# Ten float32r weight blocks of a float32 encoder trunk: the rounded copy fetched by a second transfer instead of made by ScalarE

## The chip, the core and the metric

The kernel runs on one core of one Trainium2 chip. The metric is the device time of one execution in microseconds, lower is better; a comparison uses the median over rounds. The float32r matrix products run on TensorE, whose granted clock was full in the profiled execution (0.998 of full speed over the span).

## What is computed

A bidirectional encoder of two layers works on two groups of requests with the same weights: 256 prompt tokens and 512 sample tokens, width 1024, all in float32. Both groups are handled as six tiles of 128 tokens; attention stays within its group. Each layer is a token mixer and then a SwiGLU channel mixer of inner width 2816, each between two RMS norms:

```python
for i in range(DEPTH):                                   # DEPTH = 2
    h = rms_norm(x, norm_mix_pre[i])
    if i % 2 == 0:
        m = window_gqa_sink(h, a_w_in, a_w_o, a_sinks)   # the first mixer
    else:
        m = diff_attention(h, b_w_in, b_w_o, ...)        # the second mixer
    x = x + rms_norm(m, norm_mix_post[i])
    h = rms_norm(x, norm_ffn_pre[i])
    x = x + rms_norm(swiglu(h, w_gate_up[i], w_down[i]), norm_ffn_post[i])
```

Only the first mixer matters for the change. It has 16 query heads of 64 in four groups, one key and value head per group, rotary positions on queries and keys, a window of 128 tokens to both sides, and a learned sink logit per head. For each query block of 128 tokens and each head: scores against two or three key blocks, the row maximum with the sink, the exponential, the sum with the sink's term, the division, and the product with the values; then the output projection `o @ w_o`.

## The kernel before

**Three products for one.** A weight product is computed to nearly float32 precision from float32r operands. Each operand is split into a high part, which is the operand rounded to float32r, and a low part, which is the operand minus the high part. A product is then three matmuls: high by high, high by low, low by high. In the code a block of weights has a raw tile `wraw` (float32, 128x1024), a high tile `whi` and a low tile `wlo`. `two_parts` makes them: ScalarE copies `wraw` into `whi`, which rounds, and VectorE subtracts `whi` from `wraw` into `wlo`. The activations have `hhi` and `hlo`, made in the same way, for the tiles 0 to 2 (half 0) and 3 to 5 (half 1).

**How the weights flow.** All weight blocks stand in one list in the order of use, called units. Units 0 to 3 are the weights of values and of the first keys (128x768 each). Units 4 to 12 are nine blocks of 128x1024 for eight pairs of query heads and the second pair of key heads: q0, q1, q2, q3, k8, q4, q5, q6, q7. Units 13 to 20 are the output projection; the channel mixer's units follow. `load` issues the transfer of a raw block on SyncE's queue; there are two buffers for `wraw`, and a buffer comes free when VectorE has made the low part. There are five buffers each (`RING = 5`) for `whi` and `wlo`, so unit i takes the buffer of unit i-5 and can only be written when TensorE has finished with that one. `prepare(upto)` emits the split of the units up to a number; `free` calls it when a unit's last product has been emitted.

**The order of the work.** The first mixer walks a list of projections ("fills"): values and first keys of the six tiles with q0 between, then each query block by halves, then the key block k8 by halves. Into the matmuls of the fills it places, at written positions, the attention's steps of heads already projected. A step is: scores (`sc`, TensorE), mask and row maximum (VectorE, a custom instruction that writes `y_e` and `negm`), exponential (ScalarE), reciprocal of the sum (`den`, VectorE), the scaling of two heads by it (`y_e`; one head on VectorE, one on ScalarE), transposes (`tpe`, TensorE), their copy (`eT`, ScalarE), and the product with the values (`poa`, TensorE). A projected query block is turned by its rotary positions: ScalarE copies it out of PSUM to `xqa`, two transfers issued by GpSimd exchange the rows of the two rotary halves, VectorE multiplies by the tables and adds (`zqa`), and ScalarE and VectorE split the result into `qa`. The tile framework's scheduler then sets the order of the instructions on each engine; each engine executes its instructions strictly in that order. `tc.issue_after` keeps instructions behind a named one in that order.

**GpSimd's queue** in the first mixer holds the row factors of the norms (`rstd_pre`), the exchanging transfers (`xqa`, `xka`) and the copies of a key block to the other half of the partitions (`ka`), in one order. A transfer whose condition isn't met holds whatever stands behind it.

The change touches the end of `prepare`, where every unit is split. Its line before is `two_parts(hi[:, :n], lo[:, :n], src[:, :n])`. `raw_src[r][0]` is the block's address in DRAM.

Of the kernel before, what the change touches and what calls it, by code (L numbers as in the profile page):

```python
# [9 lines left out]
F32 = mybir.dt.float32  # L10
# [3 lines left out]
ALU = mybir.AluOpType  # L14
# [9 lines left out]
NPAIR = NCH // 2  # L24
DOWN = ("b11", "t1", "t2", "b22", "t3", "t4")
RING = 5
NGRP = (NPAIR + 1) // 2
RAW = {"w": 2, "y": 2, "tt": 2, "rb": 2}
AHEAD = 6
# [58 lines left out]
def trunk(  # L88
# [22 lines left out]
    nc = tc.nc  # L111
# [22 lines left out]
    for at, step, mult in ((0, 1, -1), (2 * P, -1, 1)):  # L134
        nc.gpsimd.affine_select(
            out=mask[:, at:at + P], in_=mask[:, at:at + P], compare_op=ALU.is_ge, fill=MASK, base=0,
# [45 lines left out]
    raw_src, units = [], []  # L182
# [13 lines left out]
    def ffn_units(layer):  # L196
# [13 lines left out]
        for kind, quarter, home in (  # L210
                ("plain", (1, 0), "w"), ("b11", (0, 0), "tt"), ("t1", (0, 1), "rb"), ("t2", (1, 1), "w"),
                ("b22", (1, 1), "w"), ("t3", (1, 0), "w"), ("t4", None, None)):
            for g in range(NGRP):
                n = 512 * min(2, NPAIR - 2 * g)
# [22 lines left out]
    state = {"dma": 0, "split": 0, "used": 0, "w": 0, "y": 0, "tt": 0, "rb": 0, "behind": None, "after": None, "hold": False}  # L237
# [10 lines left out]
    def fetch(upto=None):  # L248

        while state["dma"] < (len(raw_src) if upto is None else upto):  # L250
            i = state["dma"]
            src, n, home = raw_src[i]
            if upto is None and (state[home] >= RAW[home] or home in quarters and dpool[0] is None):
                break
            if RAW["w"] <= i < 4:
                raw = first.tile([P, 768], F32, name=f"wraw{i}")
            elif home == "y":
                raw = new_y(f"wraw{i}")
            elif home in quarters:
                small_one = n < 1024  # L260
                raw = dpool[0].tile(
                    [P, n], F32, tag=home + "s" * small_one, name=f"{home}{i}", bufs=1 if small_one else NPAIR // 2)
            else:
                raw = wpool.tile([P, 1024], F32, tag="wraw", name=f"wraw{i}", bufs=RAW["w"])
            if not RAW["w"] <= i < 4:
                state[home] += 1
            load(raw[:, :n], src)
            raws[i] = raw
            state["dma"] += 1

    def two_parts(hi, lo, src):
        state["raw_hi"] = nc.scalar.copy(out=hi, in_=src)  # L272
        state["raw_lo"] = nc.vector.tensor_tensor(out=lo, in0=src, in1=hi.bitcast(F32), op=ALU.subtract)  # L273

    def prepare(upto):

        while state["split"] < min(upto, len(units)):
            i = state["split"]
            kind, r, n = units[i]
            if kind != "t4":  # L280
                fetch((r[1] if kind in ("t32", "t14") else r) + 1)
            hi = wpool.tile([P, 1024], F32R, tag="whi", name=f"whi{i}", bufs=RING)
            lo = wpool.tile([P, 1024], F32R, tag="wlo", name=f"wlo{i}", bufs=RING)
            if kind in ("plain", "gate"):
                src = raws[r]
            elif kind == "t14":
                src = raws[r[0]]
            elif kind in DOWN:
# [11 lines left out]
                src = {"b11": raw, "b22": raw, "t3": rb}.get(kind, tt)  # L300
            else:
# [10 lines left out]
                src = u  # L312
            with ExitStack() as after:
                if state["after"] is not None:
                    after.enter_context(tc.issue_after(state["after"].ins))
                if 4 <= i < 8:
                    after.enter_context(tc.issue_after(state["rstd"].ins))
                    after.enter_context(tc.issue_after(state["scaled"].ins))
                two_parts(hi[:, :n], lo[:, :n], src[:, :n])
            if kind == "t14" and units[i - 2][0] == "plain":  # L320
                state["t14_lo"] = state["raw_lo"]
            if kind == "b22":
# [22 lines left out]
    def take(n):  # L345

        i = state["used"]
        state["used"] += n
        prepare(i + n)
        return [parts.pop(j) for j in range(i, i + n)]  # L350

    def free(n_live):

        if not state["hold"]:
            prepare(state["used"] - n_live + RING)

# [779 lines left out]
    def ffn(layer, later, comb, cpool, cstack, ostack, gains):  # L1136
        sub = 2 * layer + 1
        at_hand = [
            dram.tile([P, 7, min(2, NPAIR - 2 * g), HALF], F32, name=f"act{layer}_{g}") for g in range(NGRP)]
        a_ops = {  # L1140
# [182 lines left out]
        with ExitStack() as st:  # L1323
# [53 lines left out]
            def one(p, g, into, first=False, last=False):  # L1377
                wk = {g: take(1)[0]}
                run(p, [g], wk, range(3), into, first, last)
                acts.used(1)  # L1380
                free(0)

            def whole(p, into, events):

                for g in range(NGRP):
                    one(p, g, into, p in (0, 1, 2) and g == 0, g == NGRP - 1)
                    for e in events.get(g, ()):
# [18 lines left out]
                3: [do(stage, 0, 3), do(stage, 1, 2)]}  # L1406
            for g in range(NGRP - 2):
                one(5, g, V)
                for e in events[g]:
                    e()  # L1410
            gs = range(NGRP - 2, NGRP)
            wk = dict(zip(gs, take(2)))
# [274 lines left out]
```

## Time and profile before

| | us |
|---|---|
| median of three timed runs | 1646.34 (1643.15 to 1646.58) |
| profiled execution, its own time | 1643.85 |
| its span, first to last instruction | 1642.1 |
| TensorE busy in the span | 1607.4 |
| VectorE busy | 1202.0 |
| ScalarE busy | 949.5 |
| GpSimd busy | 164.3 |

The profiled execution lies 2.5 us under the median of the timed runs and within their range. Its time is 1.75 us more than its span. In the views that follow PE is TensorE's matmuls, PEld its weight loads, DVE VectorE, ACT ScalarE, POOL GpSimd and SP SyncE; "SPq" and "POOLq" are transfers issued on those queues. A row of a timeline gives the start, the duration, the engine, the line, the operation with what it writes and reads, and in brackets how long the engine had been idle just before and what it waited for. All line numbers in profile rows are those of the kernel before.

### The profile page before, as it was taken

Reading aid. Unit: us, or ns where it says so; the run is one execution under the profiler, and the core shown is the slowest. Engines: PE = TensorE matmul, PEld = TensorE weight load, DVE = VectorE, ACT = ScalarE, POOL = GpSimd, SP = SyncE. Lnnn points to the kernel's source line nnn. Section 1 sums busy time; section 2 is a strip of 40 time slices with the busy share of each in tenths; the row PEclk is TensorE's granted clock in tenths of the full one; section 3 lists DMA queues with packets and bytes.
Section 4 is the critical chain, followed back from the end, with each engine's and each line's share of the span. In section 5 each row is a group of like instructions: output and inputs, shape, how many; then the busy total and the mean of one; then the engine's idle time right before and its main releaser. Section 6 shows DMA issues by size and latency. Waiting matters only on the chain. (4 is left out here: it accounts for less than half of the span.)

```text
span 1642.1 us, 24438 instructions
## 1 busy us (share of the span) xinstructions
PE 1607.4 (98%) x9055; PEld 1489.1 (91%) x9055; DVE 1202.0 (73%) x2076; ACT 949.5 (58%) x2009; POOL 164.3 (10%) x251
## 2 busy tenths in 40 slices
PE   7999999999999999999999999999999999999997
PEld 7888878999999998888999999888989999998886
DVE  6778857886666766988685886847886667656985
ACT  6789976644444444556475676766644444444553
POOL 1111001000000000001220251421000000000010
PEclk9999999999999999999999999999999999999999
DMA  5322205453433247666432322504443433347674
GB/s 201 97 70 58 97 15 176 170 170 111 144 111 122 100 138 269 237 235 209 130 97 71 100 72 85 148 15 178 155 158 123 144 112 103 114 143 255 215 242 159
DMA packets 71943, 227.83 MB, mean 139 GB/s; under 512 B 8912, under 2 KB 17296, under 8 KB 71568
## 3 DMA queue, kind: packets, MB, share of 16 engines
q1 hardware_dynamic: 55008, 178.82, 32.5%
q0 software_dynamic: 16672, 47.20, 9.5%
q8 instruction: 71, 1.16, 0.3%
q14 instruction: 48, 0.39, 0.1%
q10 hardware_dynamic: 144, 0.26, 0.0%
HBM read 166.47 MB, written 42.86 MB: 127 GB/s over the span
## 5 line engine op out<-in xcount | busy, mean ns | idle before, releaser
L273 DVE TENSOR_TENSOR wlo<-wraw,whi 128x1024 fp32r<-128x1024 f32 (+2 forms) x171 | 203.0, 1190 | 189.7 <-ACT whi L272 188.8
L272 ACT CAST whi<-wraw 128x1024 fp32r<-128x1024 f32 (+2 forms) x171 | 174.9, 1026 | 126.2 <-PE py L371 61.6
L370 PE MATMUL py<-hhi,whi 128*128 128x384 f32 x480 | 161.2, 336 | 1.0 <-ACT u L1177 0.9
L372 PE MATMUL py<-hhi,wlo 128*128 128x384 f32 x480 | 160.4, 334 | 0.0
L371 PE MATMUL py<-hlo,whi 128*128 128x384 f32 x480 | 160.4, 334 | 0.0
L358 ACT CAST hhi<-araw 128x768 fp32r<-128x768 f32 (+1 forms) x74 | 57.6, 783 | 93.3 <-DMA araw<-act 93.0
L370 PEld LDWEIGHTS py<-hhi,whi 128*128 128x128 f32 x480 | 90.1, 188 | 3.4 <-ACT u L1177 2.4
L372 PE MATMUL pv<-whi,hlo 128*128 128x512 f32 (+1 forms) x240 | 92.2, 384 | 0.1
L370 PE MATMUL pv<-whi,hhi 128*128 128x512 f32 (+1 forms) x240 | 92.3, 384 | 0.0
L371 PE MATMUL pv<-wlo,hhi 128*128 128x512 f32 (+1 forms) x240 | 92.1, 384 | 0.0
L371 PEld LDWEIGHTS py<-hlo,whi 128*128 128x128 f32 x480 | 90.1, 188 | 0.0
L372 PEld LDWEIGHTS py<-hhi,wlo 128*128 128x128 f32 x480 | 90.1, 188 | 0.0
L359 DVE TENSOR_TENSOR hlo<-araw,hhi 128x768 fp32r<-128x768 f32 (+1 forms) x74 | 65.2, 890 | 32.8 <-ACT hhi L358 32.5
L1220 POOL DMA_DIRECT2D act<-st x22 | 19.3, 878 | 628.6 <-DVE st L1219 628.6
L370 PE MATMUL po<-whi,hhi 128*128 128x512 f32 x192 | 78.5, 409 | 0.0
L1017 ACT ACTIVATE be<-bsc,bmx 128x512 f32<-128x512 f32 (+1 forms) x96 | 58.7, 615 | 30.4 <-DVE bmx L1015 29.8
L371 PE MATMUL px<-hlo,whi 128*128 128x384 f32 x224 | 75.0, 335 | 0.7 <-DVE hlo L359 0.7
L370 PE MATMUL px<-hhi,whi 128*128 128x384 f32 x224 | 75.3, 336 | 0.2 <-ACT hhi L358 0.2
L371 PE MATMUL po<-wlo,hhi 128*128 128x512 f32 x192 | 75.3, 392 | 0.0
L372 PE MATMUL po<-whi,hlo 128*128 128x512 f32 x192 | 75.2, 392 | 0.0
L372 PE MATMUL px<-hhi,wlo 128*128 128x384 f32 x224 | 74.9, 335 | 0.0
L1015 DVE TENSOR_REDUCE bmx<-bsc 128x1 f32<-128x512 f32 (+1 forms) x96 | 55.2, 594 | 11.3 <-PE bsc L1011 10.9
(315 smaller groups left out, 4897.9 us busy)
## 6 DMA issues: line engine op xcount, KB each, us to landing
wraw<-in_wgu SPq DMA_DIRECT2D x60, 512.0 KB, 4.5
act<-st POOLq DMA_DIRECT2D x22, 1344.0 KB, 6.5
araw<-act SPq DMA_DIRECT2D x70, 384.0 KB, 3.9
y_wraw<-in_wgu SPq DMA_DIRECT2D x40, 512.0 KB, 3.7
wraw<-in_wd SPq DMA_DIRECT2D x40, 512.0 KB, 3.7
xd<-x SPq DMA_DIRECT2D x18, 512.0 KB, 3.1
x<-xd SPq DMA_DIRECT2D x18, 512.0 KB, 4.3
wraw<-in_wo SPq DMA_DIRECT2D x16, 512.0 KB, 3.7
```

The costliest lines, as they stand in the source:

```text
L272: state["raw_hi"] = nc.scalar.copy(out=hi, in_=src)
L273: state["raw_lo"] = nc.vector.tensor_tensor(out=lo, in0=src, in1=hi.bitcast(F32), op=ALU.subtract)
L358: state["hi"] = nc.scalar.copy(out=hi, in_=src)
L359: state["lo"] = nc.vector.tensor_tensor(out=lo, in0=src, in1=hi.bitcast(F32), op=ALU.subtract)
L370: nc.tensor.matmul(out, ah, bh, start=start and i == 0, stop=False, skip_group_check=more)
L371: nc.tensor.matmul(out, ah, bl, start=False, stop=False, skip_group_check=more)
L372: state["mm"] = nc.tensor.matmul(out, al, bh, start=False, stop=stop and i == last, skip_group_check=more)
L1015: nc.vector.tensor_reduce(out=mx, in_=s, axis=AX.X, op=ALU.max, negate=True)
L1017: nc.scalar.activation(out=e[:, :n * P], in_=s, func=AF.Exp, bias=mx, accum_out=den[:, c:c + 1])
L1220: nc.gpsimd.dma_start(out=at_hand[c // 4][:, :, c // 2 % 2], in_=out.pop(c // 2))
```

## The change

For units 4 to 13 the high part is no longer made by ScalarE. GpSimd issues a second transfer of the same block from DRAM, whose destination is the float32r tile `whi`, so that the transfer itself rounds. VectorE's subtraction is as before, but now reads a `whi` that came by transfer. These are the nine blocks of queries and keys and the first block of the output projection. The raw block still comes by SyncE's transfer, since the low part needs it. All other units are split as before.

```diff
--- before.py
+++ after.py
@@ -24,6 +24,7 @@
 NPAIR = NCH // 2
 DOWN = ("b11", "t1", "t2", "b22", "t3", "t4")
 RING = 5
+N_PLAIN_A = 14
 NGRP = (NPAIR + 1) // 2
 RAW = {"w": 2, "y": 2, "tt": 2, "rb": 2}
 AHEAD = 6
@@ -316,7 +317,12 @@
                 if 4 <= i < 8:
                     after.enter_context(tc.issue_after(state["rstd"].ins))
                     after.enter_context(tc.issue_after(state["scaled"].ins))
-                two_parts(hi[:, :n], lo[:, :n], src[:, :n])
+                if 4 <= i < N_PLAIN_A:
+                    nc.gpsimd.dma_start(out=hi[:, :n], in_=raw_src[r][0])
+                    state["raw_lo"] = nc.vector.tensor_tensor(
+                        out=lo[:, :n], in0=src[:, :n], in1=hi[:, :n].bitcast(F32), op=ALU.subtract)
+                else:
+                    two_parts(hi[:, :n], lo[:, :n], src[:, :n])
             if kind == "t14" and units[i - 2][0] == "plain":
                 state["t14_lo"] = state["raw_lo"]
             if kind == "b22":
```

The scheduler sets a new order around this. In the pieces below a number in a name like `whi5` is the unit; `xqa1_0` is the rotary exchange of query block 1, half 0; `den`, `negm` and `y_e` carry group, tile and first head.

GpSimd's queue at the first query blocks, before and then now:

```order
L415 TENSOR_TENSOR rstd_pre0_5_395<-rstd_pre0_5_395,mhalf_101 128x1
L653 DMA xqa0_0_481<-xqa0_0_481 64x384 x2
L653 DMA xqa1_0_716<-xqa1_0_716 64x384 x2
L653 DMA xqa0_1_787<-xqa0_1_787 64x384 x2
L653 DMA xqa1_1_868<-xqa1_1_868 64x384 x2
L653 DMA xqa2_0_971<-xqa2_0_971 64x384 x2
L653 DMA xqa3_0_1077<-xqa3_0_1077 64x384 x2
```

```order
L421 TENSOR_TENSOR rstd_pre0_4_331<-rstd_pre0_4_331,mhalf_101 128x1
L421 TENSOR_TENSOR rstd_pre0_5_395<-rstd_pre0_5_395,mhalf_101 128x1
L659 DMA xqa0_0_481<-xqa0_0_481 64x384 x2
L321 DMA whi5_596<-in_waf 128x1024
L321 DMA whi6_615<-in_waf 128x1024
L321 DMA whi7_635<-in_waf 128x1024
L321 DMA whi8_647<-in_waf 128x1024
L659 DMA xqa1_0_716<-xqa1_0_716 64x384 x2
L321 DMA whi9_781<-in_waf 128x1024
L659 DMA xqa0_1_787<-xqa0_1_787 64x384 x2
L321 DMA whi10_862<-in_waf 128x1024
```

The ten transfers stand between the exchanges: unit 4 ahead of the third row factor (not shown), units 5 to 8 in a row ahead of the second query block's exchange, unit 9 and unit 10 one exchange later each. Further on, units 11, 12 and 13 stand ahead of the copies of the first `ka` half, of `xqa3_1` and of `xka8_1`.

TensorE where unit 5 is used for the first time, at the end of the last value projection (`pkva5`), before and then now:

```order
L372 MATMUL pkva5_589<-whi3_205,hlo1_113 128x384
L370 MATMUL pqa1_0_665<-hhi0_110,whi5_596 128x384
L371 MATMUL pqa1_0_665<-hlo0_112,whi5_596 128x384
L372 MATMUL pqa1_0_665<-hhi0_110,wlo5_597 128x384
L783 MATMUL sc0_0_1_669<-ka0_296,qa0_0_520 128x256 x2
L370 MATMUL pqa1_0_665<-hhi0_110,whi5_596 128x384
L371 MATMUL pqa1_0_665<-hlo0_112,whi5_596 128x384
L372 MATMUL pqa1_0_665<-hhi0_110,wlo5_597 128x384
```

```order
L378 MATMUL pkva5_589<-whi3_205,hlo1_113 128x384
L376 MATMUL pqa1_0_665<-hhi0_110,whi5_596 128x384
L377 MATMUL pqa1_0_665<-hlo0_112,whi5_596 128x384
L789 MATMUL sc0_0_1_669<-ka0_296,qa0_0_520 128x256 x2
L742 MATMUL tka4_683<-ident_r_86,sp4_579 128x128 x4
L789 MATMUL sc0_1_0_690<-ka0_296,qa0_0_520 128x256 x2
L378 MATMUL pqa1_0_665<-hhi0_110,wlo5_597 128x384
L376 MATMUL pqa1_0_665<-hhi0_110,whi5_596 128x384
```

The first matmul with the low part of unit 5 has moved behind two scores and a transpose.

VectorE at the same place, before and then now:

```order
L609 TENSOR_TENSOR kr4_580<-kr4_580 128x128
L273 TENSOR_TENSOR wlo5_597<-wraw5_178,whi5_596 128x1024
L729 TENSOR_TENSOR sp4_579<-kr4_580,sp4_579 128x128 x2
L792 ISA y_e0_0_0_624,negm0_0_0_625<-sc0_0_0_621,mask_91,nsink_107 128x256
L792 ISA negm0_0_0_625 128x1
L273 TENSOR_TENSOR wlo6_616<-wraw6_367,whi6_615 128x1024
L603 TENSOR_TENSOR kr5_656<-pkva5_589,cos_sb_99 128x128
L606 TENSOR_TENSOR kr5_656<-pkva5_589,sin_sb_100 128x64 x2
L792 ISA y_e0_0_0_624,negm0_0_0_625<-sc0_0_1_669,mask_91,nsink_107 128x256
L792 ISA negm0_0_0_625 128x1
L609 TENSOR_TENSOR kr5_656<-kr5_656 128x128
L801 TENSOR_TENSOR den0_0_0_626<-negm0_0_0_625,sink_106 128x2
```

```order
L615 TENSOR_TENSOR kr4_580<-kr4_580 128x128
L735 TENSOR_TENSOR sp4_579<-kr4_580,sp4_579 128x128 x2
L798 ISA y_e0_0_0_624,negm0_0_0_625<-sc0_0_0_621,mask_91,nsink_107 128x256
L798 ISA negm0_0_0_625 128x1
L322 TENSOR_TENSOR wlo5_597<-wraw5_178,whi5_596 128x1024
L609 TENSOR_TENSOR kr5_656<-pkva5_589,cos_sb_99 128x128
L612 TENSOR_TENSOR kr5_656<-pkva5_589,sin_sb_100 128x64 x2
L322 TENSOR_TENSOR wlo6_616<-wraw6_367,whi6_615 128x1024
L615 TENSOR_TENSOR kr5_656<-kr5_656 128x128
L798 ISA y_e0_0_0_624,negm0_0_0_625<-sc0_0_1_669,mask_91,nsink_107 128x256
L798 ISA negm0_0_0_625 128x1
L735 TENSOR_TENSOR sp5_655<-kr5_656,sp5_655 128x128 x2
```

`wlo5` stood ahead of `sp4` and the first maximum and now stands behind them; `wlo6` follows it closely. `wlo7` and `wlo8`, which are not shown, keep their places to within a few rows.

VectorE at unit 13, in the attention of group 1, before and then now:

```order
L659 TENSOR_TENSOR zqa3_1_1428<-zqa3_1_1428,xqa3_1_1424 128x384
L792 ISA y_e1_2_2_1499,negm1_2_2_1500<-sc1_2_2_1496,mask_91,nsink_107 128x256
L792 ISA negm1_2_2_1500 128x1
L803 TENSOR_TENSOR den1_1_2_1456<-den1_1_2_1456 128x2
L792 ISA y_e1_2_2_1499,negm1_2_2_1500<-sc1_2_3_1519,mask_91,nsink_107 128x256
L792 ISA negm1_2_2_1500 128x1
L804 RECIPROCAL den1_1_2_1456<-den1_1_2_1456 128x2
L273 TENSOR_TENSOR wlo13_1514<-wraw13_1298,whi13_1513 128x1024
L668 TENSOR_TENSOR qa3_1_1485<-zqa3_1_1428,qa3_1_1485 64x384 x2
L806 TENSOR_SCALAR y_e1_1_2_1454<-y_e1_1_2_1454,den1_1_2_1456 128x256
L792 ISA y_e1_3_0_1543,negm1_3_0_1544<-sc1_3_0_1540,mask_91,nsink_107 128x384
```

```order
L665 TENSOR_TENSOR zqa3_1_1428<-zqa3_1_1428,xqa3_1_1424 128x384
L809 TENSOR_TENSOR den1_1_2_1456<-den1_1_2_1456 128x2
L798 ISA y_e1_2_2_1499,negm1_2_2_1500<-sc1_2_3_1519,mask_91,nsink_107 128x256
L798 ISA negm1_2_2_1500 128x1
L810 RECIPROCAL den1_1_2_1456<-den1_1_2_1456 128x2
L807 TENSOR_TENSOR den1_2_2_1501<-negm1_2_2_1500,sink_106 128x2
L812 TENSOR_SCALAR y_e1_1_2_1454<-y_e1_1_2_1454,den1_1_2_1456 128x256
L674 TENSOR_TENSOR qa3_1_1485<-zqa3_1_1428,qa3_1_1485 64x384 x2
L798 ISA y_e1_3_0_1543,negm1_3_0_1544<-sc1_3_0_1540,mask_91,nsink_107 128x384
L798 ISA negm1_3_0_1544 128x1
L661 TENSOR_TENSOR zka8_1_1534<-xka8_1_1530,ropea0_238 128x384
L322 TENSOR_TENSOR wlo13_1514<-wraw13_1298,whi13_1513 128x1024
```

The scaling of `y_e1_1_2` stood behind `wlo13` and behind the split of `qa3_1`, and now stands ahead of both. `wlo12`, which is not shown, stood ahead of the scaling of `y_e1_2_0` and of both maxima of `y_e1_1_2`; now it stands behind that scaling and between the two maxima.

## The prediction

> **What bounds the kernel now.** I read first the page's head with the busy time of each engine, then the busy time by stretches (the columns are the stretch, its length, and PE, PEld, DVE, ACT and POOL busy, granted clock, DMA share, GB/s), then TensorE's waits between 20 and 200 us.
>
> ```profile
> span 1642.1 us, 24438 instructions
> ...
> PE 1607.4 (98%) x9055; PEld 1489.1 (91%) x9055; DVE 1202.0 (73%) x2076; ACT 949.5 (58%) x2009; POOL 164.3 (10%) x251
> ...
> 0.00:60.00 60.00, 51.68 (x311) 49.96 (x312) 39.23 (x96) 38.65 (x91) 7.23 (x19) 1.00 0.52 176
> 60.00:76.00 16.00, 12.63 (x81) 11.94 (x79) 14.31 (x46) 12.40 (x34) 2.20 (x4) 1.00 0.28 91
> 76.00:112.00 36.00, 35.87 (x240) 31.02 (x239) 28.12 (x97) 31.69 (x92) 5.80 (x10) 1.00 0.19 49
> 112.00:126.00 14.00, 11.83 (x77) 10.24 (x78) 11.19 (x41) 11.73 (x35) 2.20 (x4) 1.00 0.32 103
> 126.00:200.00 74.00, 72.26 (x474) 61.01 (x472) 61.02 (x213) 68.21 (x197) 10.07 (x18) 1.00 0.23 71
> 200.00:1642.10 1442.10, 1423.15 (x7883) 1324.94 (x7879) 1048.14 (x1588) 786.85 (x1565) 136.84 (x196) 1.00 0.44 144
> ...
> PE tpe L824 <- DVE y_e L806: 2.4, 3, 2.0
> PE tpe L824 <- DVE den L801: 2.1, 2, 1.9
> PE sc L783 <- DVE qa L668: 1.4, 1, 1.4
> ```
>
> TensorE bounds the kernel at full clock. The change lies in the first 200 us; the order of the instructions behind them is the old one, so a shift made there is carried to the end as it is. In those 200 us TensorE can lose or win only at places where it waits: three groups of waits hold 2.4 + 2.1 + 1.4 = 5.9 us, and all three end at VectorE. None ends at ScalarE's rounding. Between 76 and 112 us TensorE is busy for 35.87 of 36 us. So the change is worth what it moves at three places (63, 73 and 121 us), less what a late transfer costs.
>
> **The change part by part.** What goes: ten roundings of 1.05 us on ScalarE. What comes: ten transfers of 512 KB on GpSimd's queue. The subtractions stay on VectorE, but wait now for a landing.
>
> ```profile
> L272 ACT CAST whi<-wraw x10: 1031/1048/1064, 25.4 to 115.8; 128x1024 fp32r<-128x1024 f32 x10
> ...
> act<-st POOLq DMA_DIRECT2D x22, 1344.0 KB, 6.5
> kb<-kb POOLq DMA_DIRECT2D x32, 192.0 KB, 3.1
> wraw<-in_waf SPq DMA_DIRECT2D x9, 512.0 KB, 3.7
> ...
> L653 POOL DMA_DIRECT2D xqa<-xqa x32: 552/552/718, 34.8 to 195.4; - x32
> ...
> DMA to landing us min/median/max: 1.8/2.6/4.1
> ```
>
> *The landing.* No transfer that rounds 512 KB is in the trace. By GpSimd's queue 192 KB land after 3.1 us and 1344 KB after 6.5; on the line between them 512 KB land after 3.1 + 3.4 x 320/1152 = 4.0 us, close to the 3.7 us of the same block on SP's queue. I take 4.0; the ends are 3.1 (rounding and size cost nothing) and 6.5 (it costs as much as the largest transfer). Where the rounding has another price it is a rival below. Ten issues at 0.55 to 0.72 us of GpSimd time are 5.5 to 7.2 us; GpSimd is busy for 7.23 + 2.20 + 5.80 + 2.20 + 10.07 = 27.5 of 200 us, and that idle time hides them: 0. The exchanges behind them in its queue wait for a copy of a query block, which comes later than the release of the buffer in every place that the order shows; without that cover each exchange would be late by one issue, 0.7 us.
>
> *Unit 5, TensorE at 48 us.* The rows are ScalarE's rounding of unit 5 and TensorE's first use.
>
> ```profile
> 44.60 1.05 ACT L272 CAST whi<-wraw 128x1024 fp32r<-128x1024 f32 x1 [0.67 <-PE pkva L372]
> 48.14 0.33 PE L370 MATMUL pqa<-hhi,whi 128*128 128x384 f32 x1
> 50.46 0.46 PE L736 MATMUL tka<-ident_r,sp 128*128 128x128 f32 x4
> 50.76 0.47 PE L783 MATMUL sc<-ka,qa 128*128 128x256 f32 x2
> 51.07 0.34 PE L370 MATMUL pqa<-hhi,whi 128*128 128x384 f32 x1
> ```
>
> The rounding waited for TensorE to release the buffer (44.60). The transfer is released at the same moment and lands at 44.6 + 4.0 = 48.6, 0.46 after TensorE wants it: **+0.5**. The subtraction (1.22, quoted below) then ends at 49.8. Until its first use TensorE now has two products with the high part (0.17 each from start to start), two scores and a transpose (0.30 and 0.31 from the starts above): 1.27 us, which covers it. With 3.1 us the term is 0, with 6.5 it is 44.6 + 6.5 - 48.14 = +3.0. What is late next is the end of query block 1, half 0, and with it the exchange on which the wait at 63 us hangs, so I count the delay in full.
>
> *Units 9 and 10, TensorE at 63 and 73 us.* ScalarE and VectorE rows around the two waits:
>
> ```profile
> 60.97 1.05 ACT L666 CAST qa<-zqa 64x384 fp32r<-64x384 f32 x2 [1.39 <-DVE zqa L659]
> 61.26 1.22 DVE L273 TENSOR_TENSOR wlo<-wraw,whi 128x1024 fp32r<-128x1024 f32 x1
> 62.04 0.49 ACT L651 ACTIVATE xqa<-pqa 128x384 f32<-128x384 f32 x1
> 63.11 0.51 PE L783 MATMUL sc<-ka,qa 128*128 128x256 f32 x2 [1.45 <-DVE qa L668]
> 65.65 1.03 ACT L272 CAST whi<-wraw 128x1024 fp32r<-128x1024 f32 x1
> 66.76 0.56 DVE L658 TENSOR_TENSOR xqa<-xqa,ropea 128x384 f32<-128x384 f32 x1 [1.39 <-DMA xqa<-xqa]
> 68.11 1.22 DVE L273 TENSOR_TENSOR wlo<-wraw,whi 128x1024 fp32r<-128x1024 f32 x1
> 70.53 0.48 DVE L792 CUSTOM_DVE_ANT_0 y_e<-sc,mask,nsink 128x256 f32<-128x256 f32 x1
> 73.39 0.64 PE L824 MATMUL tpe<-ident,y_e 128*128 128x128 f32 x4 [1.92 <-DVE den L801]
> ```
>
> The subtraction of unit 9 (61.26) stood ahead of the split of `qa1_0`, which could begin at 62.48. It now stands four rows behind that split's group, in the gap of 1.39 ahead of 66.76. The split can begin when ScalarE's rounding ends, 62.02: 0.46 earlier. The gap, longer by that, is 1.85 and takes the 1.22, so the row at 66.76 comes 0.63 earlier if its exchange has landed. It will have: its copy (62.04) now stands ahead of the rounding of `qa1_0`, where ScalarE idled for 1.39. The wait at 73 us follows VectorE, busy 14.31 of 16 us here, so both waits together give **-0.6**. The subtraction of unit 10 stood at 68.11 and now stands behind two maxima (0.48 each) and a split (1.14): 70.2 - 0.6 = 69.6. Its buffer is free at 65.65 at the latest and the block lands at 69.65: 0. With 6.5 it lands at 72.15, and VectorE, with everything behind it in its order, is 2.6 us late, TensorE too.
>
> *Units 12 and 13, TensorE at 121 us.* VectorE, ScalarE and TensorE rows:
>
> ```profile
> 115.76 1.05 ACT L272 CAST whi<-wraw 128x1024 fp32r<-128x1024 f32 x1 [0.17 <-PE pqa L371]
> 116.61 0.56 DVE L658 TENSOR_TENSOR xqa<-xqa,ropea 128x384 f32<-128x384 f32 x1 [1.80 <-DMA xqa<-xqa]
> 118.63 1.21 DVE L273 TENSOR_TENSOR wlo<-wraw,whi 128x1024 fp32r<-128x1024 f32 x1
> 118.69 0.33 PE L370 MATMUL pqa<-hhi,whi 128*128 128x384 f32 x1
> 119.22 0.34 PE L370 MATMUL pqa<-hhi,whi 128*128 128x384 f32 x1
> 119.87 1.14 DVE L668 TENSOR_TENSOR qa<-zqa,qa 64x384 fp32r<-64x384 f32 x2
> 121.04 0.35 DVE L806 TENSOR_SCALAR y_e<-y_e,den 128x256 f32<-128x256 f32 x1
> 121.54 0.63 PE L824 MATMUL tpe<-ident,y_e 128*128 128x128 f32 x4 [1.99 <-DVE y_e L806]
> ```
>
> The scaling at 121.04 stood behind the subtraction of unit 13 and a split and now stands ahead of both: 121.04 - (121.04 - 118.63) = 118.63. The subtraction of unit 12 goes later, into the gap of 1.80 ahead of 116.61. The transposes start 0.5 after the scaling does, as before: 119.15 instead of 121.54. TensorE was ready at 121.54 - 1.99 = 119.55 and is now ready four matmuls earlier (three take 119.22 - 118.69 = 0.53, four 0.7), at 118.85. A wait of 0.3 stays: **-1.7**. The release of unit 13's buffer is at 115.76, its landing at 119.8, and its subtraction now stands behind 118.63 + 0.35 + 1.14 and more, past 120: 0. What goes back: the next transposes wait for the scaling of `y_e1_2_2`, which now stands behind that subtraction (1.21); and behind 126 us ScalarE is busy for 68.21 of 74 us, so that TensorE, early, finds work that isn't ready. Nothing in the trace says how much; between 0 and 1.7 I take half: **+0.85**.
>
> *ScalarE's ten microseconds.* Seven of the ten roundings end before 67 us, where ScalarE is busy for 38.65 of 60 and 12.40 of 16 us; the other three are at 100 to 116 us, where the waits end at VectorE. What they free is idle time, beyond the order already counted: 0; rival two prices it otherwise. *Memory.* The second reading adds 5.2 MB. The DMA share is 0.52 up to 60 us and 0.19 to 0.32 up to 200; the room left hides it, and no wait of TensorE quoted above ends at a transfer: 0, or, without that room, the longer landing already bounded.
>
> The sum: 0.46 - 0.63 - 1.7 + 0.85 = -1.0. With 3.1 us and nothing given back it is -0.63 - 1.7 = -2.3; with 6.5 it is 3.0 - 0.63 + 2.6 - 1.7 + 0.85 = +4.1. The profiled execution took 1643.85 us by its own time, so it becomes 1642.9; the median of the runs is 2.5 us above it, so the forecast on the median is 1646.34 - 1.0 = **1645.4**, from 1644.0 to 1650.4 by the ends.
>
> **The rivals.** *One, slower: the rounding transfer is slow.* If it rounds at half the speed of the plain block, it lands after 2 x 3.7 = 7.4 us. Then unit 5 holds TensorE at 48 us for 44.6 + 7.4 - 48.14 = 3.9, and unit 10 holds VectorE at 73 us for 65.65 + 7.4 - 69.6 = 3.5, with the scalings and splits behind it: 3.9 + 3.5 - 0.63 - 1.7 + 0.85 = +5.9, 1652.2. Each further microsecond costs two, so from a landing of 6.2 us on the result is slower by more than 3.3. For it: no row shows a transfer with rounding, and units 5 and 10 have no slack left at 4.0 us (-0.46 and -0.05). Against it: the plain rows, at 3.7 and 6.5.
>
> *Two, faster: ScalarE's relief counts.* From 60 to 200 us ScalarE is busy for 12.40 + 31.69 + 11.73 + 68.21 = 124.0 of 140 us, and what VectorE waits with often comes from it (exponentials, roundings of a split). If its shorter queue gives back three quarters of the 5.9 us of waits, it is -4.4: 1641.9. Against it: those waits are named as VectorE's, and seven of ten roundings stood in idle time.
>
> *Three: the gain is handed on whole.* If the work behind 126 us holds TensorE until the old time, and units 5 and 10 cancel, nothing is left: 1646.3.
>
> [...]
>
> **How the numbers follow.** 0.2%, 3.3 us, is about what a measurement of this kernel can tell from no change. The forecast gets 0.36, rival one 0.22, two 0.25, three 0.12, four 0.05. Faster is rival two, 0.25; slower is rival one, 0.22; the rest, 0.53, is within 0.2%. The forecast's own range is 1644.0 to 1650.4. The range for all takes in rivals one and two about to their prices, so that some 0.2 stays outside: 1641.0 to 1652.2.
>
> **What would show it.** In the changed kernel's trace: ten transfers of `whi` with a landing near 4 us (rival one: 6.2 or more); TensorE's wait for `whi` at 48 us near 0.5; waits at 63 and 73 us of 1.45 and 1.92 together shorter by about 0.6; the transposes of 121 us with a wait of 0.3 instead of 1.99, and new waits of about 0.9 in all between 124 and 200 us. A busy time of TensorE that changes, or a difference behind 200 us, would mean that the argument looked in the wrong place.

## The result, and the profile after

The changed kernel takes 1641.95 us in the median, against 1645.84 us for the kernel before (22 runs each). The ratio is 0.998 with a 95% interval of 0.9974 to 0.9986: 3.3 us faster, between 2.3 and 4.3. One run of the changed kernel was disturbed (2676 us) and is not in the ratio. The forecast was -1.0 us. Its own range, 1644.0 to 1650.4 us, did not hold the time; the range that takes in the rivals, from 1641.0 us on, did. The end of this section and the last experiment show that 2.1 us of the gain, about two thirds, come from a place that the prediction did not look at.

The page's head, TensorE's waits between 20 and 210 us, and the busy time by stretches of the changed kernel (columns as before):

```profile
span 1641.9 us, 24431 instructions
...
PE 1610.2 (98%) x9055; PEld 1491.5 (91%) x9055; DVE 1200.9 (73%) x2076; ACT 941.0 (57%) x1999; POOL 170.9 (10%) x261
...
PE tpe L830 <- DVE y_e L812: 2.3, 2, 2.1
PE tpe L830 <- ACT y_e L813: 1.0, 3, 0.4
PE poa L845 <- ACT eT L836: 0.8, 2, 0.4
PE sc L789 <- DVE qa L674: 0.6, 1, 0.6
PE pqa L376 <- DMA whi<-in_waf: 0.5, 1, 0.5
...
60.00:76.00 16.00, 13.36 (x82) 12.75 (x81) 14.14 (x47) 11.74 (x35) 4.24 (x8) 0.94 0.60 206
74.00:77.50 3.50, 3.35 (x12) 3.38 (x13) 2.54 (x11) 3.45 (x10) 1.09 (x2) 0.51 0.35 132
112.00:126.00 14.00, 13.32 (x86) 11.97 (x85) 12.11 (x43) 10.89 (x34) 2.89 (x6) 1.00 0.53 157
126.00:200.00 74.00, 72.49 (x474) 61.30 (x473) 61.13 (x214) 68.67 (x199) 9.94 (x18) 1.00 0.23 72
```

The span is only 0.2 us shorter than in the profile of before, although the timed runs differ by 3.3. The profiled execution of before (1643.85 us) lies 2.0 under that kernel's median. This one (1643.67 us) is 1.7 over its own, and the row from 74 to 77.5 us gives one reason: there the granted clock was 0.51. A single pair of traces can't carry the comparison here. Rows have to be matched place by place.

The rows of TensorE and VectorE at the places of the prediction:

```profile
49.58 0.41 PE L376 MATMUL pqa<-hhi,whi 128*128 128x384 f32 x1 [0.47 <-DMA whi<-in_waf]
63.73 0.51 PE L789 MATMUL sc<-ka,qa 128*128 128x256 f32 x2 [0.56 <-DVE qa L674]
74.15 1.09 PE L830 MATMUL tpe<-ident,y_e 128*128 128x128 f32 x4 [2.08 <-DVE y_e L812]
120.57 0.60 PE L830 MATMUL tpe<-ident,y_e 128*128 128x128 f32 x4
122.82 1.22 DVE L322 TENSOR_TENSOR wlo<-wraw,whi 128x1024 fp32r<-128x1024 f32 x1 [0.72 <-DMA whi<-in_wo]
...
L659 POOL DMA_DIRECT2D xqa<-xqa x32: 527/545/657, 35.6 to 196.0; - x32
...
DMA to landing us min/median/max: 3.8/5.1/5.8
```

The first exchange starts at 35.6 us instead of 34.8. This lead of 0.8 us of the kernel before is there from 16 us on, before any product uses a changed unit, so it isn't the change: by the clock records of the two traces the full clock was granted 1.8 us later in this execution (16.0 against 14.2 us). Counted without it, the scores at 63 us come 0.2 us earlier than before (63.73 against 63.11), the transposes at 73 us at the same time (74.15 against 73.39), and the transposes at 121 us no longer wait at all (120.57 against 121.54). The last row is the time from issue to landing of the ten new transfers: 5.1 us in the median, not 4.0.

The half-clock stretch begins at 74.0, at the end of a wait of 2.08 us, and costs about 1.5 us: the shift against the kernel before grows from 0.8 at 74 us to 2.2 at 80. Among the fourteen traces of this study such a stretch stands at this place in four (the changed kernel twice, order_only, combo6), behind 121 us in one, and nowhere in the first mixer in the other nine. It lasts 3.41 us each time. Waits of much the same length brought it in some executions and not in others: the 2.08 us here did, the 1.99 us at 121 us in the trace of before did not. The part on the clock below shows when.

The last two outputs of the kernel before, and then of the changed kernel:

```profile
1636.25 0.34 SPq L564 DMA_DIRECT2D ys<-x  x1
1636.92 0.37 ACTq L564 DMA_DIRECT2D ys<-x  x1
```

```profile
1638.20 0.34 SPq L570 DMA_DIRECT2D ys<-x  x1
1638.87 0.37 ACTq L570 DMA_DIRECT2D ys<-x  x1
```

From the issue of the last output to the end of the span it was 1642.1 - 1636.9 = 5.2 us; now it is 1641.9 - 1638.9 = 3.0. No instruction there was changed. This is 2.1 us, the larger part of the gain. The traces also hold instructions that the views don't count as busy, and these name what is last. Near the program's end every engine executes instructions called DRAIN. GpSimd's long one, its closing drain, began at 1634.2 us and took 7.05 in the kernel before; it ended 2.3 us behind the landing of the last output (1639.0), and the span ended 0.8 us behind the drain. In the changed kernel it took 1.50 us and ended at 1637.7, ahead of the landing of the last output (1640.9), and the span ended 1.0 us behind that landing.

### The profile page after: what moved, and what is told of

Its sections match the earlier page's. It is cut to its first block, busy times and chain, and to the rows that moved or that the text cites. A ratio compares the mean times of both kernels' runs of the same rounds, so it can differ in the third digit from the quotient of the medians.

```text
span 1641.9 us, 24431 instructions
## 1 busy us (share of the span) xinstructions
PE 1610.2 (98%) x9055; PEld 1491.5 (91%) x9055; DVE 1200.9 (73%) x2076; ACT 941.0 (57%) x1999; POOL 170.9 (10%) x261
## 2 busy tenths in 40 slices
DMA packets 73383, 233.07 MB, mean 142 GB/s; under 512 B 9072, under 2 KB 17456, under 8 KB 73008
## 5 line engine op out<-in xcount | busy, mean ns | idle before, releaser
L274 DVE TENSOR_TENSOR wlo<-wraw,whi 128x1024 fp32r<-128x1024 f32 (+1 forms) x161 | 190.7, 1188 | 188.4 <-ACT whi L273 187.4
L273 ACT CAST whi<-wraw 128x1024 fp32r<-128x1024 f32 (+1 forms) x161 | 164.3, 1024 | 130.7 <-PE py L377 61.5
```

## The experiments

Four theories are named in the expectations. A: the gain comes from VectorE's order at unit 13, so that the wait at 121 us falls. B: it comes from ScalarE's relief, by the number of roundings removed. C: a wait of two microseconds costs a second time through the granted clock. D, formed late: the end of the program depends on GpSimd's transfers. The shifts below are those of the same operation on TensorE against the profile of before (negative is earlier), matched by the order of the operations:

| kernel | 40 us | 60 us | 70 us | 90 us | 128 us | 205 us | last output to end |
|---|---|---|---|---|---|---|---|
| changed | +0.8 | +1.5 | +0.6 | +2.3 | +0.9 | +0.6 | 3.0 |
| changed, second trace | +0.9 | +1.7 | +0.6 | +3.0 | +2.4 | +2.2 | 3.0 |
| late3 | -0.1 | -0.2 | -0.1 | +0.1 | -1.2 | -1.2 | 3.0 |
| early7 | +1.0 | +1.6 | +0.8 | +1.0 | +1.2 | +1.4 | 3.0 |
| order_only | +0.8 | +0.8 | +0.8 | +2.5 | +2.0 | +1.9 | 5.2 |
| before, three more traces | +0.4, +1.0, +0.5 | +0.4, +1.0, +0.5 | +0.4, +1.0, +0.5 | +0.6, +0.9, +0.7 | +0.4, +2.2, +0.3 | +0.3, +2.1, +0.3 | 5.2, 5.2, 5.4 |

**Which units bring the gain.** The first run transfers units 11 to 13 only (the edit is shown against the changed kernel):

```diff
-                if 4 <= i < N_PLAIN_A:
+                if 11 <= i < N_PLAIN_A:
```

> Only units 11, 12 and 13 come by the second transfer; units 4 to 10 are rounded by ScalarE as before. Theory A, the gain comes from the order of VectorE at unit 13 (the scaling of y_e1_1_2 ahead of the low part and of the split): TensorE's wait of 1.99 us at 121.5 falls below 0.5, the waits of 1.45 and 1.92 at 63 and 73 us stay, and the time is 2 to 4 us below the kernel before, the whole gain of the change. Theory B, ScalarE's relief counts by the number of roundings removed: three of ten, so 1 to 1.2 us below the kernel before.

It took 1642.31 us, ratio 0.9979 (0.9970 to 0.9989): -3.5 us, as much as the whole change. Up to 112 us nothing moved; at 121 us the wait was gone and the shift went from 0.0 to -1.2, and stayed. Its waits:

```profile
PE tpe L830 <- DVE den L807: 2.1, 1, 2.1
PE sc L789 <- DVE qa L674: 1.6, 1, 1.6
PE tpe L830 <- ACT y_e L813: 1.0, 3, 0.4
PE tpe L830 <- DVE y_e L812: 1.0, 3, 0.4
PE poa L845 <- ACT eT L836: 0.6, 2, 0.4
```

The waits of 63 and 73 us are the old ones. So theory A holds in its place; but A expected the whole gain at 121 us, and there are only 1.2 of 3.5. Those 1.2 are also what theory B expected of three roundings, so this run alone doesn't decide against B. The other half transfers units 4 to 10 only (`if 4 <= i < 11`).

> Only units 4 to 10 come by the second transfer; 11 to 13 are rounded by ScalarE as before. Theory A: the wait at 121.5 us stays near 2, TensorE waits about 0.5 for the high part of unit 5, the wait at 63 us is shorter by about 0.9, and the time is within 1 us of the kernel before. Theory B: seven of ten roundings are gone, so 2.3 to 2.7 us below it.

It took 1645.01 us, ratio 0.9989 (0.9978 to 0.9999): -1.8 us, with an interval from -3.6 to -0.2, although TensorE was 0.4 us later at 205 us than at 40. With seven roundings gone, the first mixer as a whole was no faster, where theory B expected 2.3 to 2.7 us. Its waits at 49 us (0.3 for the landing) and 63 us (0.7) are near what was expected; the one at 121 us stayed and was longer (2.6). Where the timed gain came from wasn't explained at this point.

The third run makes no transfer and holds back only one instruction, VectorE's low part of unit 13 (`state["scaling"]` is a name given to VectorE's scaling in another line, not shown). Around it the scheduler set a new order on TensorE, VectorE and ScalarE between 118 and 152 us:

```diff
-                two_parts(hi[:, :n], lo[:, :n], src[:, :n])
+                if i == 13:
+                    state["raw_hi"] = nc.scalar.copy(out=hi[:, :n], in_=src[:, :n])
+                    with tc.issue_after(state["scaling"].ins):   # the scaling of y_e1_1_2
+                        state["raw_lo"] = nc.vector.tensor_tensor(...)
+                else:
+                    two_parts(hi[:, :n], lo[:, :n], src[:, :n])
```

> The kernel before, no second transfer and all ten roundings on ScalarE; only VectorE's low part of unit 13 is held behind the scaling of y_e1_1_2. Theory A: the wait of 1.99 us at 121.5 falls below 0.7 and the time is 1.5 to 3.5 us below the kernel before. Theory B: no rounding is removed, so no change (within 0.7 us).

It took 1643.15 us, ratio 0.9987 (0.9978 to 0.9996): -2.1 us, from -3.6 to -0.7. The wait of 1.99 us became one of 0.4, as expected, but TensorE won only 0.5 at 121 us (+2.5 to +2.0): small waits of 0.2 to 0.4 us stand in its place, for ScalarE's scaling, its copies, and the next scalings. So the order removes the wait, but what TensorE keeps of it, 0.5 us, is no more than the 0.3 to 0.6 by which traces without any change there move (they follow below). That late3 keeps 1.2 may go with ScalarE's three roundings at 100 to 116 us, with unit 12's place, or with the noise of two traces; no run parts these. The timed gain of 2.1 us is larger than the traced one, and the end is as long as before (5.2 us); the clock, below, is a candidate for the rest.

**What a transfer that rounds costs.** Raw blocks by GpSimd's queue, without rounding, all roundings on ScalarE:

```diff
-            load(raw[:, :n], src)
+            load(raw[:, :n], src, nc.gpsimd if 4 <= i < 14 else nc.sync)
```

(`load` takes the queue as a new argument; that line is not shown.)

> The kernel before with the raw blocks of units 4 to 13 issued by GpSimd and not by SyncE, without rounding, and all roundings on ScalarE: a price for a plain 512 KB transfer on GpSimd's queue. If rounding costs the transfer time, the plain landings have a median near 3.7 us, against the 5.1 us of the rounding ones; if it is the queue and the size, the plain ones have a median near 5 us too. The time itself decides nothing here, since the order on GpSimd changes.

```profile
wraw<-in_waf POOLq DMA_DIRECT2D x9, 512.0 KB, 3.9
```

On the same queue the plain block lands after 3.9 us, and the rounding ones had a median of 5.1 (4.9 in late3, 5.0 in early7). This difference is not the price of rounding. In the changed kernel each block is fetched twice, and the plain raw blocks land late, too. The rows are the busy time from 45 to 57 us of the kernel before and of the changed one, the raw blocks of the changed one, and the landings of two groups of its rounding transfers: units 6 to 9, which move beside each other or beside raw blocks, and units 11 and 12, which have no other weight block beside them:

```profile
45.00:57.00 12.00, 12.00 (x80) 11.93 (x79) 9.08 (x27) 9.02 (x25) 1.10 (x2) 1.00 0.47 140
45.00:57.00 12.00, 11.53 (x73) 11.17 (x72) 6.47 (x22) 4.75 (x17) 2.62 (x5) 1.00 0.80 260
...
wraw<-in_waf SPq DMA_DIRECT2D x9, 512.0 KB, 4.9
...
DMA to landing us min/median/max: 5.3/5.6/5.8
...
DMA to landing us min/median/max: 3.8/3.9/4.0
```

Units 11 and 12 have that freedom in five traces (the changed kernel twice, late3, late3_warm, combo6). These ten rounding transfers landed after 3.6 to 4.9 us, 3.9 in the median, as the plain ones did. So no run shows a price of rounding; the late landings go with several blocks on the way at once, and the DMA share rose from 0.47 to 0.80 where four of them stood in a row. The kernel of this run took 1641.54 us in its one execution, although it removes no rounding. Its stretch from the last output to the end is 3.2 us.

**Does a wait cost a second time, by the clock?** The half-clock stretches suggested it, and the mean granted clock of the timed runs was higher in the faster kernels. One run puts idle products into the two longest waits of the kernel before (the transposes are held behind them in the same way; that part of the edit is not shown):

```diff
+                if (g, t, j) in ((0, 0, 3), (1, 1, 3)):
+                    idle = bank(f"idle{g}_{t}_{j}")[:, :HALF]
+                    for c in range(WARM[g]):                     # 10 and 14
+                        with tc.issue_after(state["mm"].ins):
+                            state["mm"] = nc.tensor.matmul(
+                                idle, h_hi[0][:, c % KT, :P], h_hi[0][:, c % KT], start=True, stop=True)
```

> The kernel before, with ten and fourteen float32r products of 128x384 into a bank that nobody reads, put on TensorE directly ahead of the transposes that wait at 73 and at 121 us; they fill the waits and take no wait away. Theory C: a wait of two microseconds costs a second time, because the granted clock is halved for a stretch of 3.4 us after it in many executions. Then the mean granted clock of the timed runs rises from 0.9975 (the kernel before) to 0.9985 or more and the time falls by 1 to 2.5 us, although nothing up to 200 us starts earlier. Without C: the time is the same or up to 0.5 us longer.

1645.34 us, ratio 1.0001 (0.9989 to 1.0012). The idle products did not fit the waits: at 73 us 1.3 us of waiting were left behind them, at 121 us they ran longer than the wait, and TensorE was 1.4 us late by 205 us; the time is the old one. The mean granted clock rose from 0.9972 only to 0.9979, not to 0.9985. The same filling at 73 us on top of late3:

> Units 11 to 13 by the second transfer, and ten idle products ahead of the transposes that wait at 73 us. Theory C: the mean granted clock is at least 0.9988 and the time 0.5 to 1.5 us below that of late3, 4 to 5 us below the kernel before. Without C: as late3, 3.3 us below the kernel before, or up to 0.5 longer.

1641.95 us, ratio 0.9979 (0.9970 to 0.9988): as late3. Neither run shows the gain that theory C expected. But neither refutes C: TensorE came to 205 us 1.4 us later in warm, and in late3_warm it won nothing between 40 and 205 us where late3 won 1.1, and yet the times are the old ones. Something gave about as much back. Three more traces of the kernel before looked for the stretch itself:

> The kernel before, unchanged, for a second trace. Its mean granted clock over the timed runs is 0.0011 to 0.0012 below that of the changed kernel, about one stretch of 3.4 us at half clock more per execution. Theory C (in the form in which the wait of 1.99 us at 121 us causes it): this trace shows a granted clock near 0.5 to 0.8 in the first few us behind 121 us, with probability two in three. Rival: the half-clock stretches lie elsewhere (behind 73 us, or at the passages between the layers' parts near 320, 750 and 1150 us), which are the same in both kernels.

> The kernel before, unchanged, for a third trace; the same expectations: under theory C a granted clock well below 1 just behind 121 us with probability two in three, under the rival elsewhere.

> The kernel before, unchanged, for a fourth trace; the same expectations: under theory C a granted clock well below 1 just behind 121 us with probability two in three, under the rival elsewhere.

The three runs took 1644.82, 1649.17 and 1645.51 us. Only the second has a half-clock stretch, and it stands behind 121 us; stretches of before_b:

```profile
112.00:123.00 11.00, 9.03 (x56) 8.30 (x54) 9.08 (x30) 9.11 (x27) 1.94 (x4) 0.97 0.34 112
123.00:126.40 3.40, 3.40 (x15) 2.13 (x15) 1.34 (x8) 2.33 (x8) 0.27 (x1) 0.60 0.17 61
126.40:130.00 3.60, 3.60 (x26) 2.87 (x25) 2.77 (x10) 3.00 (x9) 0.00 (x0) 1.00 0.01 2
```

It begins behind a wait of 1.88 us, which ended at 122.2 us, and costs 1.3 us (the shift goes from +0.9 at 90 us to +2.2 at 128). So a wait of about two microseconds cost a second time in this execution, and not in the other three of the same kernel.

The traces also show in which. The half-clock stretches begin and end on a grid of 3.413 us, which lies differently in each execution: counted from the first grant of the full clock, at 15.98 us in the changed kernel's trace and at 14.18 in that of before, the later changes of the clock come after 17, 18 and 475 steps of it in the one and after 475 in the other. Of all windows of this grid ahead of the program's end, in the fourteen traces, six have TensorE idle for 1.93 to 2.65 us (by the modelled ends of its products); each is followed by a window at half clock. Of two with 1.88 us one is, and of those with 1.82 us or less none. In the changed kernel 1.93 of the 2.08 us at 73 us fall in the window that ends at 74.0. In the trace of before the grid parts the 1.99 us at 121 us, with 1.55 us in the fuller window, and the clock stays full (1.00). An estimate from these figures, with 1.85 us in one window as the border: the 1.99 us of the kernel before halve the clock in (3.41 + 1.99 - 2 x 1.85) / 3.41, half of all executions, and cost some 0.7 us on average.

Four traces of before and two of the changed kernel are too few to tell what this is worth in the comparison. The mean granted clock misled in part: the mean runs over the whole span, and behind 1636 us TensorE has nothing to do and runs at half clock (0.50 in the kernel before), so that a kernel whose end is 2.1 us shorter shows a mean that is higher by 0.0006. Yet warm and order_only, whose end is as long as before, show 0.0007 and 0.0008 more than the kernel before, and 0.0007 of 1645 us are 1.2 us; late3 and the changed kernel show 0.0012, late3_warm 0.0017; early7 and three_more, which keep the wait at 121 us, only 0.0003 and 0.0004 (each to about 0.0005). This fits a part of the gain that comes by the clock, from the wait at 121 us that is gone or filled. No run isolates it.

Side by side the traces point to another place, the end itself (the last column of the table): with more GpSimd transfers it was about 2.1 us shorter in every trace so far (3.0 to 3.3 us against 5.1 to 5.4), whatever the first mixer did.

**The changed kernel again, and a mixture.**

> The changed kernel again, for a second trace of it and its time on the same chip as the others. Theories A and C: 3 to 4 us below the kernel before; mean granted clock 0.998 to 0.999; TensorE's first product behind 200 us starts 1.2 to 2.2 us earlier than in the kernel before when the late start of the full clock and each half-clock stretch (about 1.5 us each) are taken off.

1641.35 us, ratio 0.9981 (0.9972 to 0.9990): -3.1 us, as before. Its second trace shows what the first one hid, in rows of VectorE and TensorE:

```profile
124.31 1.23 DVE L322 TENSOR_TENSOR wlo<-wraw,whi 128x1024 fp32r<-128x1024 f32 x1 [1.57 <-DMA whi<-in_wo]
126.25 0.35 DVE L812 TENSOR_SCALAR y_e<-y_e,den 128x256 f32<-128x256 f32 x1
126.66 0.44 PE L830 MATMUL tpe<-ident,y_e 128*128 128x128 f32 x2 [0.90 <-DVE y_e L812]
```

Unit 13's transfer, issued at 118.57 us, landed late, VectorE stood 1.57 us at its subtraction, and the next scaling and the next transposes behind it were late: from 90 to 205 us this execution won 0.8 us, where the first won 1.7. Up to 205 us it won about 0.3 when the late start of the clock and the half-clock stretch are taken off; 1.2 to 2.2 was expected.

The mixture transfers units 11 to 13 as late3 does and has GpSimd issue the raw blocks of units 6 to 10 (only this second part of the edit is shown):

```diff
-            load(raw[:, :n], src)
+            load(raw[:, :n], src, nc.gpsimd if 6 <= i < 11 else nc.sync)
```

> Units 11 to 13 by the second transfer; the raw blocks of units 6 to 10 issued by GpSimd, the roundings of units 4 to 10 on ScalarE. In the kernel with raw blocks on GpSimd the wait at 73 us was gone (0.5 instead of 1.9); if that came from the units from 6 on, TensorE waits nowhere above 0.7 us after 20 us but at 63, and the time is 4.5 to 6 us below the kernel before. If it came from units 4 and 5, it is as late3, 3.3 us below.

1638.65 us (5 runs), ratio 0.9965 (0.9952 to 0.9977): -5.8 us, from -7.9 to -3.8. This is the fastest kernel of the study, some 2.5 us under the changed one, with intervals that overlap. The reason expected was wrong: the wait at 63 us went away and the one at 73 us stayed. That the time fell as forecast is luck: TensorE won 0.8 us from 40 to 205 us and the end 1.8, and the rest of the 5.8 lies behind 205 us, where the order is the old one and where two executions of the kernel before also part by 3 us (before_b goes from +2.1 to +5.3). Whether it would last is not shown.

```profile
PE tpe L830 <- DVE den L807: 2.1, 1, 2.1
PE tpe L830 <- ACT y_e L813: 1.0, 3, 0.5
PE poa L845 <- ACT eT L836: 0.9, 2, 0.5
PE tpe L830 <- DVE y_e L812: 0.8, 2, 0.4
```

**The end of the kernel.** The last run is the kernel before with three tiny transfers added on GpSimd's queue, whose data nobody reads. It changes nothing else in the first mixer: the order on every other engine is that of the kernel before.

```diff
+            for i in range(3):
+                extra = small.tile([P, 8], F32, tag="extra", name=f"extra{i}", bufs=3)
+                nc.gpsimd.dma_start(out=extra, in_=xp[:P, 8 * i:8 * i + 8])
```

> The kernel before with three tiny transfers (128x8, read by nobody) added on GpSimd's queue at its start; no other engine's order changes. In the traces so far the stretch from the last output's issue on ScalarE's queue to the end of the span is 5.1 to 5.3 us in all six executions of kernels with the old number of GpSimd transfers (158), and 3.0 to 3.3 us in all seven with 161 to 168. Theory D: that stretch depends on GpSimd's transfers as such, not on what they carry. Then here (161) it is 3.0 us, TensorE's waits at 63, 73 and 121 us stay as before, and the time is 2.1 us below the kernel before (1 to 3). Rival: it depends on the transfers that round, on their size or on the first mixer's order; then the stretch is 5.1 us and the time that of the kernel before.

```profile
span 1638.8 us, 24441 instructions
...
PE tpe L824 <- DVE y_e L806: 2.4, 3, 2.0
PE tpe L824 <- DVE den L801: 1.9, 1, 1.9
PE sc L783 <- DVE qa L668: 1.7, 1, 1.7
...
1635.75 0.37 ACTq L564 DMA_DIRECT2D ys<-x  x1
```

1643.56 us, ratio 0.9986 (0.9976 to 0.9995): -2.3 us, from -3.9 to -0.8. All three waits of the first mixer are there, and the end is 1638.8 - 1635.75 = 3.05 us. Theory D holds: 2.1 us of the gain go with GpSimd's closing drain, 7.05 us in all six traces with 158 GpSimd transfers (4 of the kernel before, order_only, warm) and 1.3 to 1.5 in all eight with 161 to 168. Here it made no difference whether the transfers round, nor how large they are: the end is 3.05 us with three plain ones of 4 KB and 3.0 with ten rounding ones of 512 KB. Why 158 is slow and 161 is not, and whether other counts are slow, no run shows. With the 2.1 us early7 is accounted for, too: 0.4 later and 2.1 earlier make -1.7, and -1.8 was measured.

## Why the prediction was right, and where it was wrong

*The sum and what was measured.* The first mixer was forecast at -1.0 us. Without the late start of the clock and the half-clock stretches, the two traces of the changed kernel give about -1.7 and -0.3 up to 205 us. With the 2.1 us of the end, the sum is -2.4 to -3.8, and the timed gain is -3.3 (-4.3 to -2.3) and -3.1 (-4.6 to -1.6). So the predicted mechanism is there, at about the size of the forecast, and makes about a third of the gain. Its size is known poorly: three traces without any change there (before_a, before_c, three_more) also moved by 0.1 to 0.5 us in the same direction between 40 and 205 us, against the same trace of before.

*The time.* The forecast's own range, from 1644.0 us on, did not hold the 1641.95. The wide range held it because it reached down to rival two, and the time lies on that rival's price, 1641.9, by luck: its reason, ScalarE's relief, is not what the runs show. (1646.34 - 1.0 is 1645.3, not the 1645.4 of the forecast; nothing hangs on it.)

*The step that failed* is the sentence that behind 200 us the order is the old one, "so a shift made there is carried to the end as it is". Order was taken for time. The new transfers are ten more entries in GpSimd's queue, and GpSimd's closing drain, 7.05 us in the kernel before and 1.50 in the changed one, lay on the path that set the end of the kernel before. The shift itself was carried: late3 is 1.2 us early at 205 us and 1.4 at 1600. But the prediction counted ten issues and their neighbours, and not the drain. Its own last part named the case, a difference behind 200 us, as the sign that it looked in the wrong place.

*The landing* was sized at 4.0 us by a line through transfers that don't round. The line was right (3.9 plain, and 3.9 in the median for rounding ones with no other block beside them). What the median of 5.1 has more goes with the term called *Memory*, put at 0 because the DMA share of 0.52 leaves room: with each block fetched twice, the share from 45 to 57 us rose to 0.80 and both copies landed late (the raw one after 4.9 us in the median instead of 3.7). The bound of 6.5 us held it.

*Unit 5, +0.5.* TensorE waited 0.47 us for it. The size came out by errors that cancel: the transfer of unit 5 landed 3.8 us after its issue, 0.2 less than taken, but it was issued 0.3 us later than the release that the prediction took.

*Units 9 and 10, -0.6.* The waits at 63 and 73 us are 0.56 and 2.08 instead of 1.45 and 1.92: 0.7 us less in all. From 40 to 73 us the shift was unchanged (+0.8 to +0.8); -0.2 was forecast for units 5, 9 and 10 together.

*Units 12 and 13, -1.7, and +0.85 given back.* The wait of 1.99 us went, with no rest where 0.3 was expected. Net, six executions with units 11 to 13 changed, or unit 13 only reordered, won 0.6 to 1.7 us from 90 to 205 us; three without (three_more, before_a, before_c) moved by 0.3 to 0.6 in the same direction. All are held against the same trace of before, so about 0.4 of each figure may belong to that trace. The forecast was 0.85. The way in which it is given back is in part the one that was named, the scaling of `y_e1_2_2` behind the subtraction of unit 13: TensorE waited 0.90 us for it in one trace, and in the other only 0.23, for ScalarE's scaling next to it. New waits of 0.9 in all were forecast between 124 and 200 us; TensorE's waits there are 1.2 and 2.2 us in the two traces, against 1.6 before.

*ScalarE, 0.* early7 removes seven roundings and wins nothing up to 205 us (rival two, at least for these seven). For the three late ones a part stays open, as order_only shows.

*Rival one* falls: a rounding transfer with no other block beside it lands as a plain one does, and the median of all, 5.1 us, is under the 6.2 from which that rival decides. *Rival three*, the gain handed on whole, falls with late3, whose shift stands to 1600 us. *Rival four*, given 0.05, is not shown: plain blocks on GpSimd's queue land after 3.9 us, and the issues of the ten transfers took 530 to 716 ns.

## What to carry to other kernels

Follow every queue that a change fills to the end of the program, not only to its last neighbour: here GpSimd's closing drain lay there, 7.05 us before and 1.50 after, and the 2.1 us that the end won were worth more than the waits that the change was costed by. Where a gain of 0.2% is at stake, match the same operation across several traces before reading a cause from one pair; two executions of one kernel differed by 2.1 us at 205 us here, by the clock's late start and one half-clock stretch. A transfer that rounds on its way took the place of an engine's copy here, and it landed as a plain one did when it had no other block beside it (3.9 us). But it fetches the same bytes a second time (233.07 MB moved in all instead of 227.83): put such transfers where few others move (beside other blocks they landed after 5.3 to 5.8 us), and where the consumer stands late, since a late landing held what stood behind it on its engine (VectorE stood 1.57 us at unit 13, and TensorE 0.90 us at the transposes that follow).

## What the runs showed of the hardware

- GpSimd's closing drain: 7.05 us with 158 GpSimd transfers in the program, 1.33 us with 161, 1.42 with 165 and 166, 1.50 with 168. The end of the span moved with it by 2.1 us.
- Rounding float32 to float32r within a transfer of 512 KB: 3.9 us to landing in the median of ten with no other weight block beside them (3.6 to 4.9), against 3.9 for the plain block on the same queue. Units 6 to 9, issued beside other blocks, took 5.3 to 5.8 us in the changed kernel.
- The granted clock was halved for 3.41 us behind a wait of about 2 us of TensorE (2.08 us in the changed kernel, 1.88 in before_b), in some executions and not in others of the same kernel (1.99 us in the first trace of before), and that cost 1.3 to 1.6 us. In fourteen traces it followed every window of 3.413 us in which TensorE was idle for 1.93 us or more (six), one of two with 1.88, and none with 1.82 or less. A mean clock over the span also contains the end, where TensorE is idle (0.50 from 1635.5 us on in the kernel before).
